# A transformer block in one kernel: low and high limbs of x and ctx in common tiles, one 512-column operand in the first projections

## The chip, the cores and the metric

The kernel runs on one core of a Trainium2 chip. The metric is the device time of one execution in microseconds (us); for the kernel before it is the median of three runs. Engines are named as in the profile: PE is TensorE (PEld its weight loads), DVE VectorE, ACT ScalarE, POOL GpSimd, and SP the queue that issues most loads.

## The reference, cut to what matters

One layer of a latent generator, D = 2048, 256 latent tokens x and 256 context tokens ctx, all in fp32:

```python
sh1, sc1, gt1, sh2, sc2, gt2 = split(silu(c) @ w_mod + b_mod, 6)      # the same of c_ctx for ctx: csh1, csc1
h  = rmsnorm(x,   g_attn) * (1 + sc1)  + sh1
hc = rmsnorm(ctx, g_attn) * (1 + csc1) + csh1
cq, ckv, kr, qn, kn, vn, f = split_columns(h  @ w_in)     # 512, 512, 64, 512, 512, 512, 512 columns
..., ckv_c, kr_c, ..., kn_c, vn_c, ... = split_columns(hc @ w_in)
o_mla = attention of 8 heads, queries from cq, keys and values from ckv, kr and ckv_c, kr_c
o_na  = neighbourhood attention of 4 heads, qn on kn, vn in a window with bias, and on kn_c, vn_c
o_fn  = fourier_mix(f, w_fnet)
x = x + gt1 * (concat(o_mla, o_na, o_fn) @ w_out)
h2 = rmsnorm(x, g_ffn) * (1 + sc2) + sh2
x = x + gt2 * conv_ffn(h2, w_up, conv_w, conv_b, w_down)
return rmsnorm(x, g_final)
```

Keys and values are needed of both streams, queries and Fourier input of x alone. So the columns of kn, ckv and kr are projected for x and ctx together, those of qn, cq and f for x alone.

## The kernel before, in words

**Limbs.** Every fp32 product is made of fp32r matmuls. A value is held as a high limb H (a cast) and a low limb L (the rest), and `mm3` (L116) issues three matmuls: H·H, H·L, L·H, at L117, L118 and L119. `split` (L129) makes the limbs: the cast on ACT (L132), the difference on DVE (L133). Weights come from HBM as fp32 `raw` tiles of 1 MB and are split in two halves into `hl` tiles; there are three buffers of half a tile (tag hl, `limb_tile` L168).

**Order of the weights.** `order` (L139) lists the tiles: the first modulation (m, two per kt) and A, then V 0 to 3, B 0 to 9, F 0 to 3, and those of MLA, of the output projection and of the feed-forward part. `take` (L197) hands out quarter tiles; it splits `look` quarters ahead and has the DMA of each tile issued some tiles ahead (`emit_dma`, L173, on SP). A `raw` tile is a buffer of tag **b8**, of which there are 12 (8 KB per partition, L69). A new b8 tile waits until a buffer is free; the trace shows them handed out in the order in which the program asks. Tag **h8** (L72) has 4 more of that size.

**Stages.**
- *A*, L440 to L464: for each of 16 kt (blocks of 128 rows of D), the modulation's shift and scale (`mod1_mm`, L361, 32 matmuls at L371; transposed at L383), from these the modulated input of the next kt (`mod1_h`, L378), and products of the last kt with 7 column blocks of w_in into 7 PSUM banks (`g1`, L412). Each bank has 512 columns: 256 tokens of x, then 256 of ctx. `mod1_h` makes for x and then for ctx: h on DVE (L404), H on ACT (L405), L on DVE (L406). `hx[m]` holds H and L of x for four kt, [128, 2, 4, 256], in h8; `hc[m]` the same of ctx, in b8. So one block and one kt take six matmuls of 256 columns (L418, L419).
- *V*, `proj_N` (L489): vn of all four groups of 128 tokens, with the tokens as stationary operand and 512 columns of weights streaming.
- *B0, B1*, `proj_T` (L478) with `both`: the last block of ckv, and kr; again 256 + 256 columns (L485, L487). After B1 ctx's input is not used any more, and `hc` is free.
- *Neighbourhood stage*, L643 to L665, seven iterations j: qn of head j (B2 to B5, x alone), from j = 4 cq (`cq_unit`, B6 to B8, then B9), scores (`na_scores`, L625, with a bias T from four small loads that are issued on SP behind the last weight tile asked for, L630), softmax, transposes (`pt_stage`, L590, PE L593) into PT, and PT times vn (`pv_stage`, L597) into mix. `qn` and each `PT` are b8 tiles; so are knH, knL, ckv, vnH, vnL, cq, mix.
- *F*, L707 to L715: f from hx; then the Fourier part mixed with the first products of MLA, MLA's eight heads, the output projection (L867), the feed-forward part.

**The second modulation** (`m2_*`, L226 to L301) is filled in between: gt1, sh2, sc2, gt2 as a sum over 16 kt of weights [128, 1024] times a scalar on DVE (L253 and L255), loaded from POOL's queue (L240). `M2` (L227) orders its eight blocks: gate 1 (blocks 0, 1), sc2 (4, 5), sh2 (2, 3), gate 2 (6, 7). `paced` (L123), called in each `mm3` with its columns, decides when a fill comes. At the end of a gate's block the sum is split and added up over partitions on PE (L287, L288) and to the bias on DVE (L291); the gate's tile is a b8 buffer, loaded on SP (L284) when its first block is summed. For sc2 and sh2 there are eight small matmuls (L277) and a copy. `fill_to(32)` after the first block of output columns (L872) makes sure that gate 1 is there.

The lines that say the most:

```python
def mm3(ps, lH, lL, rH, rL, first, last, skip=False):
    ...
    paced(3 * rH.shape[-1])
...
mm3(accs[i][:, :SEQ], lH, lL, *hsl(hx, kt), first=(kt == 0), last=(kt == KT - 1), skip=True)
g1_last.append(mm3(accs[i][:, SEQ:], lH, lL, *hsl(hc, kt), first=False, last=(kt == KT - 1), skip=True))
```

Of the kernel before, what the change touches and what calls it, by code (L numbers as in the profile page):

```python
# [8 lines left out]
F32R = mybir.dt.float32r  # L9
# [5 lines left out]
P = 128  # L15
D = 2048
KT = 16
# [22 lines left out]
def _columns(*parts):  # L40

    at, o = {}, 0
    for n, w in parts:
        at[n] = (o, o + w)
        o += w
    return at, o
# [2 lines left out]
SM, SM_W = _columns(("ident", 128), ("c1", 16), ("gq", 4), ("gkv", 4), ("gffn", 16), ("bsh2", 16), ("bsc2", 16),  # L49
                    ("conv", 352))  # L50
SA, SA_W = _columns(("c2", 32), ("bm1", 64), ("ga", 32))


@with_exitstack
def block_kernel(ctx: ExitStack, tc: tile.TileContext, a, out):
# [60 lines left out]
    def mm3(ps, lH, lL, rH, rL, first, last, skip=False):  # L116
        pe.matmul(ps, lH, rH, start=first, stop=False, skip_group_check=skip)  # L117
        pe.matmul(ps, lH, rL, start=False, stop=False, skip_group_check=skip)  # L118
        ins = pe.matmul(ps, lL, rH, start=False, stop=last, skip_group_check=skip).ins  # L119
        paced(3 * rH.shape[-1])  # L120
        return ins

    def paced(n):  # L123
        pace[1] += pace[0] * n * 0.427e-3
        if pace[1] >= 1:
            pace[1] -= 1
            fill()
# [96 lines left out]
    gates = {}  # L224

    KIND = ("g", "sh", "sc", "g")  # L226
    M2 = [(blk, kt) for blk in (0, 1, 4, 5, 2, 3, 6, 7) for kt in range(KT)]  # L227
    m2 = {"dma": 0, "acc": 0, "t": {}, "due": None, "age": 0}

    def m2_dma(n):  # L230
# [122 lines left out]


    hx, hc = [None] * 4, [None] * 4
    wt = {}
    bm1 = smv("bm1").rearrange("p (g s j) -> p g s j", g=KT, s=2)
    ga = smv("ga").rearrange("p (g j) -> p g j", g=KT)
# [19 lines left out]
    def mod1_h(kt, sb):  # L378
        with ExitStack() as held:
            for made in g1_last[-1:] if kt else x_made[1:]:  # L380
                held.enter_context(tc.issue_after(made))
            for s in range(2):
                pe.transpose(ms[:, 256 + s * P : 256 + (s + 1) * P], sb[:, s * P : (s + 1) * P], idt)  # L383
            t = tiny(4, "mt")
            tv = t.rearrange("p (s j) -> p s j", s=2)
            quarters_ = ms[:, 256:512].rearrange("p (s r c) -> p s c r", s=2, r=4)[:, :, 0:2, :]
            dve.tensor_reduce(tv, quarters_, AX.X, ALU.add)
        dve.tensor_tensor(tv, tv, bm1[:, kt], ALU.add)
        dve.scalar_tensor_tensor(tv[:, 1], tv[:, 1], 1.0, ga[:, kt], ALU.add, ALU.mult)
        m = kt // 4  # L390
        xk = xT[m][:, kt % 4, :]
        with ExitStack() as held:
            if kt:
                held.enter_context(tc.issue_after(hmade[-1]))
            dve.tensor_tensor(xk, xk, rxb, ALU.mult)
        if hx[m] is None:
            hx[m] = h8([P, 2, 4, SEQ], F32R, s="hx")
            hc[m] = b8([P, 2, 4, SEQ], F32R, s="hc")
        for j, hh in enumerate((hx, hc)):
            xs = xT[m][:, kt % 4, j * SEQ : (j + 1) * SEQ]  # L400
            A, B = tv[:, 1, j : j + 1], tv[:, 0, j : j + 1]
            H, L = hh[m][:, 0, kt % 4, :], hh[m][:, 1, kt % 4, :]
            h32 = b1(s="h32")
            hmade.append(dve.tensor_scalar(h32, xs, A, B, ALU.mult, ALU.add).ins)  # L404
            hx_made.append(act.activation(H, xs, AF.Identity, bias=B, scale=A).ins)  # L405
            dve.tensor_tensor(L, h32, H.bitcast(F32), ALU.subtract)  # L406

    def hsl(hh, kt, lo=0, n=SEQ):
        t = hh[kt // 4]
        return t[:, 0, kt % 4, lo : lo + n], t[:, 1, kt % 4, lo : lo + n]  # L410

    def g1(kt, tiles):  # L412
        for i in tiles:
            if i in (0, 4):
                wt["A"] = take(("A", kt // 2), 2 * (kt % 2) + i // 4)
            w, c0 = wt["A"], (i % 4) * P
            lH, lL = w[:, 0, c0 : c0 + P], w[:, 1, c0 : c0 + P]
            mm3(accs[i][:, :SEQ], lH, lL, *hsl(hx, kt), first=(kt == 0), last=(kt == KT - 1), skip=True)  # L418
            g1_last.append(mm3(accs[i][:, SEQ:], lH, lL, *hsl(hc, kt), first=False, last=(kt == KT - 1), skip=True))  # L419

    def a_limbs(kt, made):

# [55 lines left out]
    def proj_T(key, ps, both, part=None):  # L478

        for kt in range(*((0, KT), (0, KT // 2), (KT // 2, KT))[0 if part is None else part + 1]):  # L480
            k = kt % 4
            if k == 0:
                t = take(key, kt // 4)
            lH, lL = t[:, 0, k * P : (k + 1) * P], t[:, 1, k * P : (k + 1) * P]
            mm3(ps[:, :SEQ], lH, lL, *hsl(hx, kt), first=(kt == 0), last=(kt == KT - 1), skip=True)  # L485
            if both:
                mm3(ps[:, SEQ:], lH, lL, *hsl(hc, kt), first=False, last=(kt == KT - 1), skip=True)  # L487

    def proj_N(kind, toks):  # L489

# [150 lines left out]


    pace[0] = RATES["NA"]  # L643
    qn = b8([P, 2, 4, SEQ], F32R, s="qn")
    es, PTs = {}, {}
    for j in range(7):
        if j < 4:
# [8 lines left out]
        if 1 <= j < 5:  # L656
            es[j - 1] = na_scores(j - 1)
        if 2 <= j < 6:
            PT = PTs[j - 2] = b8([P, 2, 4, SEQ], F32R, s="PT")
            for qt in range(2):  # L660
                pt_stage(es[j - 2][qt], PT, qt)
            es.pop(j - 2)
# [204 lines left out]
    for nb in range(4):  # L867
# [1 line left out]
            if nb or q == 3:  # L869
                wo_unit(nb, q, t_outer=(nb == 3 and q == 3))  # L870
        if nb == 0:
            fill_to(32)  # L872
        for t in range(2):
            x2_cols(nb, t, gates[0], ss2)
        if nb == H_AT:
# [279 lines left out]
```

## Time and profile before

| | |
|---|---|
| median of 3 runs | 1261.91 us (1261.33 to 1263.05) |
| profiled execution | 1260.39 us |
| its span, first to last instruction | 1258.6 us, granted clock 0.995 |
| matmuls, weight loads | 7522 each |
| A stage | from 28 us; V from 144.5, B0 from 189.4, B2 from 212.5, F from 278.4 us |
| loads | 304.76 MB, mean 242 GB/s |

The page gives the busy time of each engine, the chain of work that ended last, groups of instructions by line, and the loads. Other views of the trace are named by what they show: windows (busy time in stretches), the timeline, waits, groups by form. Matmuls overlap, so that the mean of a group is longer than the step from one matmul to the next.

### The profile page before, as it was taken

The page shows a single profiled execution, that of the slowest core. Times are in us where ns is not written, and L with a number is a line of the kernel's source. Part 1 is how long each engine was busy: PE and PEld are TensorE (multiplying, and loading weights), DVE is VectorE, ACT ScalarE, POOL GpSimd, SP SyncE. Part 2 cuts the span into 40 slices and gives each one's busy share as a digit, 9 for nine tenths or more (in the row PEclk, how much of TensorE's full clock was granted, in tenths as well). Part 3 has the DMA queues.
Part 4 walks back from the last instruction along what each step waited for, and adds up shares of the span by engine and source line. Part 5 has one row for each costly group of instructions (what it writes and reads, how often), then busy time and mean ns, then how long its engine had stood idle before and what let it go on. Part 6 is the DMA issues. An engine that isn't in the chain of part 4 may idle for free.

```text
span 1258.6 us, 18991 instructions
## 1 busy us (share of the span) xinstructions
PE 1232.7 (98%) x7522; PEld 1073.0 (85%) x7522; DVE 956.3 (76%) x1408; ACT 634.3 (50%) x976; POOL 113.6 (9%) x175
## 2 busy tenths in 40 slices
PE   5999999999999999999999999999999999999996
PEld 4888889898888888999888888888888888888885
DVE  5455888897999788998888975777766677667785
ACT  4332323664566545666656433555543555445553
POOL 0000121011211112110121500000000000000000
PEclk8999999999999999999999999999999999999999
DMA  9999888674657798744677866555555545555541
GB/s 371 399 395 385 344 300 323 228 289 154 223 204 281 271 377 305 283 168 168 209 261 253 300 230 256 198 173 196 186 186 198 190 178 201 185 187 195 173 197 67
DMA packets 55369, 304.76 MB, mean 242 GB/s; under 512 B 6256, under 2 KB 7408, under 8 KB 29040
## 3 DMA queue, kind: packets, MB, share of 16 engines
q1 hardware_dynamic: 36128, 235.29, 50.9%
q0 software_dynamic: 18432, 67.12, 15.1%
q8 instruction: 59, 0.97, 0.3%
q10 hardware_dynamic: 720, 1.13, 0.2%
q14 instruction: 30, 0.25, 0.1%
HBM read 301.42 MB, written 2.10 MB: 241 GB/s over the span
## 4 chain that ended last, share of the span: by engine, by line
PE 93%; DVE 4%; DMA 1%; ACT 1%; issue 1%; POOL 0%; SPq 0%; DVEq 0%; POOLq 0%; ACTq 0%
PE ps L942 21%; PE ps L118 16%; PE ps L119 16%; PE ps L117 16%; PE ps L943 11%; PE g L117 2%; PE ms L371 2%; PE g L118 2%; PE g L119 2%; DMA x<-in_ctx_dram 1%; PE ps L593 1%; DVE acc L255 1%; DVE hl L133 1%; PE ps L277 1%; DVE xT L331 0%
## 5 line engine op out<-in xcount | busy, mean ns | idle before, releaser
L132 ACT CAST hl<-raw 128x1024 fp32r<-128x1024 f32 (+3 forms) x351 | 363.5, 1036 | 349.7 <-PE ps L119 242.5
L133 DVE TENSOR_TENSOR hl<-raw,hl 128x1024 fp32r<-128x1024 f32 (+3 forms) x351 | 422.0, 1205 | 154.1 <-ACT hl L132 153.6
L942 PE MATMUL ps<-hn,hl 128*128 128x512 f32 x1152 | 405.5, 397 | 0.0
L943 PE MATMUL ps<-hn,hl 128*128 128x256 f32 x1152 | 322.6, 280 | 0.0
L942 PEld LDWEIGHTS ps<-hn,hl 128*128 128x128 f32 x1152 | 216.4, 188 | 53.1
L943 PEld LDWEIGHTS ps<-hn,hl 128*128 128x128 f32 x1152 | 217.3, 189 | 0.1
L255 DVE SCALAR_TENSOR_TENSOR acc<-wm,c,acc 128x1024 f32<-128x1024 f32 x120 | 153.5, 1279 | 6.7 <-DMA wm<-in_wm_dram 6.3
L118 PE MATMUL ps<-hl,act 128*128 128x512 f32 x344 | 133.9, 389 | 0.0
L117 PE MATMUL ps<-hl,act 128*128 128x512 f32 x344 | 133.9, 389 | 0.0
L119 PE MATMUL ps<-hl,act 128*128 128x512 f32 x344 | 133.8, 389 | 0.0
L240 POOL DMA_DIRECT2D wm<-in_wm_dram x128 | 68.2, 533 | 336.4 <-DVE acc L255 247.8
L118 PEld LDWEIGHTS ps<-hl,act 128*128 128x128 f32 x344 | 64.6, 188 | 13.5 <-DVE hl L133 0.2
L117 PEld LDWEIGHTS ps<-hl,act 128*128 128x128 f32 x344 | 64.6, 188 | 13.5
L119 PEld LDWEIGHTS ps<-hl,act 128*128 128x128 f32 x344 | 64.6, 188 | 13.3
L119 PE MATMUL ps<-h,hl 128*128 128x258 f32 x256 | 72.8, 284 | 0.0
L117 PE MATMUL ps<-h,hl 128*128 128x258 f32 x256 | 72.4, 283 | 0.0
L118 PE MATMUL ps<-h,hl 128*128 128x258 f32 x256 | 72.2, 282 | 0.0
L963 ACT ACTIVATE cv<-ps,sm 128x256 f32<-128x256 f32 x88 | 49.8, 567 | 44.5 <-DVE ps L961 43.9
L235 POOL COPY hold<-hl 128x1 f32<-128x1 f32 x36 | 38.1, 1058 | 242.0 <-DVE hl L133 172.8
L964 DVE SCALAR_TENSOR_TENSOR cv<-ps,sm,cv 128x255 f32<-128x255 f32 x88 | 42.1, 480 | 20.0 <-ACT cv L963 20.0
L114 POOL TENSOR_TENSOR r<-v,mhalf 128x1 f32<-128x1 f32 (+1 forms) x3 | 2.7, 895 | 531.5 <-DVE v L113 527.7
L117 PE MATMUL ps<-hl,mix 128*128 128x512 f32 x128 | 50.4, 394 | 0.0
(287 smaller groups left out, 2238.4 us busy)
## 6 DMA issues: line engine op xcount, KB each, us to landing
raw<-in_wup_dram SPq DMA_DIRECT2D x88, 1024.0 KB, 4.9
wm<-in_wm_dram POOLq DMA_DIRECT2D x128, 512.0 KB, 5.3
raw<-in_wdn_dram SPq DMA_DIRECT2D x44, 1024.0 KB, 4.9
raw<-in_wm_dram SPq DMA_DIRECT2D x32, 1024.0 KB, 9.1
raw<-in_wo_dram SPq DMA_DIRECT2D x16, 1024.0 KB, 7.8
raw<-in_wB_dram SPq DMA_DIRECT2D x10, 1024.0 KB, 10.2
raw<-in_wA_dram SPq DMA_DIRECT2D x16, 448.0 KB, 8.4
raw<-in_wV_dram SPq DMA_DIRECT2D x4, 1024.0 KB, 10.4
```

The source lines that it names most:

```text
L117: pe.matmul(ps, lH, rH, start=first, stop=False, skip_group_check=skip)
L118: pe.matmul(ps, lH, rL, start=False, stop=False, skip_group_check=skip)
L119: ins = pe.matmul(ps, lL, rH, start=False, stop=last, skip_group_check=skip).ins
L132: act.copy(H, src)
L133: return dve.tensor_tensor(L, src, H.bitcast(F32), ALU.subtract).ins
L235: hold = pool.tensor_copy(tiny(1, "hold"), recent[0][:, 1, 0:1].bitcast(F32)).ins
L240: pool.dma_start(w, a["wm2"][blk * 16 + kt])
L255: dve.scalar_tensor_tensor(m2["a"], w, c1[:, kt : kt + 1], m2["a"], ALU.mult, ALU.add)
L942: pe.matmul(ps, w[:, 0, k * P : (k + 1) * P], h[:, k].rearrange("p s n -> p (s n)"), start=kt == 0, stop=False, skip_group_check=True)
L943: pe.matmul(ps[:, :SEQ], w[:, 1, k * P : (k + 1) * P], h[:, k, 0, :], start=False, stop=kt == KT - 1, skip_group_check=True)
L963: act.activation(t, ps[:, :SEQ], AF.Identity, bias=c[:, 3:4], scale=c[:, 1:2])
L964: dve.scalar_tensor_tensor(t[:, 1:], ps[:, : SEQ - 1], c[:, 0:1], t[:, 1:], ALU.mult, ALU.add)
```

## The change

The input of the first projections is kept by limb instead of by stream. For each m there are two tiles, `hH` (h8) and `hL` (b8), each [128, 2, 4, 256] with the stream as second index; `hx[m]` and `hc[m]` become views on them (class `Limbs`), and `hsl2` gives the 2 x 256 columns of both streams as one operand. `g1` and `proj_T` with `both` call `mm3` once for 512 columns; `proj_T` for x alone, V and F go through the views as before. `paced` counts the columns of the result.

`hL` holds x's low limb too, so its b8 buffers stay in use to the end of F. `qn` and `PT` take ctx's parts of these tiles (both limbs), after B1 is done with them: qn that of m = 3, PT in turn those of m = 0, 1, 2. In the second modulation sc2's blocks come ahead of gate 1's, and `fill_to(32)` becomes `fill_to(64)`.

```diff
+class Limbs:
+    def __init__(self, H, L):
+        self.limbs = H, L
+
+    def __getitem__(self, at):
+        return self.limbs[at[1]][(at[0],) + tuple(at[2:])]
...
-        paced(3 * rH.shape[-1])
+        paced(3 * ps.shape[-1])
...
-    M2 = [(blk, kt) for blk in (0, 1, 4, 5, 2, 3, 6, 7) for kt in range(KT)]
+    M2 = [(blk, kt) for blk in (4, 5, 0, 1, 2, 3, 6, 7) for kt in range(KT)]
...
+    hxc = [None] * 4
...
-            hx[m] = h8([P, 2, 4, SEQ], F32R, s="hx")
-            hc[m] = b8([P, 2, 4, SEQ], F32R, s="hc")
+            hxc[m] = h8([P, 2, 4, SEQ], F32R, s="hH"), b8([P, 2, 4, SEQ], F32R, s="hL")
+            hx[m], hc[m] = [Limbs(*(t[:, j] for t in hxc[m])) for j in range(2)]
...
+    def hsl2(kt):
+        return [t[:, :, kt % 4, :] for t in hxc[kt // 4]]
...
-            mm3(accs[i][:, :SEQ], lH, lL, *hsl(hx, kt), first=(kt == 0), last=(kt == KT - 1), skip=True)
-            g1_last.append(mm3(accs[i][:, SEQ:], lH, lL, *hsl(hc, kt), first=False, last=(kt == KT - 1), skip=True))
+            g1_last.append(mm3(accs[i], lH, lL, *hsl2(kt), first=(kt == 0), last=(kt == KT - 1), skip=True))
...
-            mm3(ps[:, :SEQ], lH, lL, *hsl(hx, kt), first=(kt == 0), last=(kt == KT - 1), skip=True)
             if both:
-                mm3(ps[:, SEQ:], lH, lL, *hsl(hc, kt), first=False, last=(kt == KT - 1), skip=True)
+                mm3(ps, lH, lL, *hsl2(kt), first=(kt == 0), last=(kt == KT - 1), skip=True)
+            else:
+                mm3(ps[:, :SEQ], lH, lL, *hsl(hx, kt), first=(kt == 0), last=(kt == KT - 1), skip=True)
...
-    qn = b8([P, 2, 4, SEQ], F32R, s="qn")
+    qn = hc[3]
...
-            PT = PTs[j - 2] = b8([P, 2, 4, SEQ], F32R, s="PT")
+            PT = PTs[j - 2] = hc[(j - 2) % 3]
...
-            fill_to(32)
+            fill_to(64)
```

## The prediction

> **What bounds the kernel now.** I read the page's busy times and chain first.
>
> ```profile
> PE 1232.7 (98%) x7522; PEld 1073.0 (85%) x7522; DVE 956.3 (76%) x1408; ACT 634.3 (50%) x976; POOL 113.6 (9%) x175
> PE 93%; DVE 4%; DMA 1%; ACT 1%; issue 1%; POOL 0%; SPq 0%; DVEq 0%; POOLq 0%; ACTq 0%
> ```
>
> TensorE is busy nearly throughout and carries 93% of the chain, so what the change takes from its stream in the first projections is kept, unless something else becomes late there. The windows tell what that could be (columns: window, length, busy of PE, PEld, DVE, ACT, POOL with instruction counts, clock, DMA share, GB/s).
>
> ```profile
> 28.00:60.00 32.00, 31.69 (x324) 26.95 (x328) 16.71 (x42) 10.08 (x19) 0.00 (x0) 0.95 1.01 414
> 60.00:90.00 30.00, 30.00 (x324) 25.32 (x316) 13.69 (x35) 8.74 (x15) 2.84 (x6) 1.00 0.98 387
> 310.00:350.00 40.00, 39.27 (x214) 32.97 (x212) 39.57 (x65) 21.11 (x42) 7.39 (x14) 1.00 0.68 227
> ```
>
> In the A stage, which begins at 28 us, PE is full and the transfers are nearly so: two limits lie close together. From 310 to 350, in the Fourier part and the first heads of MLA, VectorE is 99% busy (39.57 of 40) and PE loses 0.7 us: there a third one is near.
>
> **Term 1, half as many matmuls.** The groups by form count what is joined (one row of the six of the A stage and of the three of ctx in B0 and B1; x and ctx, and L117, L118 and L119, have the same counts):
>
> ```profile
> L117 PE MATMUL g<-hx,hl 128*128 128x256 f32 x112 | 34.6, 314 | 1.8 <-ACT hx L405 1.8
> L117 PE MATMUL ps<-hc,hl 128*128 128x256 f32 x32 | 9.1, 283 | 0.0
> ```
>
> 3 x 112 pairs in the A stage and 3 x 32 in B0 and B1 become one matmul of 512 columns each: 432 matmuls and 432 weight loads go. Durations overlap, so the price is the step from start to start: first B0 (16 steps lie between the two rows), then V, where 512 columns stream already (6 steps).
>
> ```profile
> 189.78 0.28 PE L117 MATMUL ps<-hc,hl 128*128 128x256 f32 x1
> ...
> 191.70 0.28 PE L118 MATMUL ps<-hx,hl 128*128 128x256 f32 x1
> ```
>
> ```profile
> 166.76 0.39 PE L117 MATMUL ps<-hl,hx 128*128 128x512 f32 x1
> ...
> 168.12 0.39 PE L117 MATMUL ps<-hl,hc 128*128 128x512 f32 x1
> ```
>
> 1.92/16 = 0.120 us for 256 columns and 1.36/6 = 0.2267 us for 512. A pair costs 0.240 now and 0.2267 afterwards: 13.3 ns less. 432 x 0.0133 = 5.75 us, of which 336 x 0.0133 = 4.47 in A and 1.28 in B. V's 512 columns are one run, the new operand is two runs of 256 in one tile; the trace has no such operand. Bounds: 0 (two runs cost what two matmuls cost) and 5.75. I take 5.75, since the step in V goes with the column count, and 256 extra columns cost 0.107.
>
> The Trainium skill (TensorE: Matmul & The Clock Gate, section on the back-to-back issue gap) gives a warm step of N/2.4 + 2.5 ns; by that a pair would save 2.5 ns and the change 1.1 us in all. The two rows do not agree: both steps lie 11 ns or more above the rule, and their difference leaves 13.3 ns per matmul.
>
> **Term 2, the start.** The first matmul now needs the high limbs of both streams.
>
> ```profile
> 28.16 0.59 ACT L405 ACTIVATE hc<-xT,mt 128x256 fp32r<-128x256 f32 x1
> 28.31 1.22 PE L117 MATMUL g<-hx,hl 128*128 128x256 f32 x4 [1.85 <-ACT hx L405]
> 29.64 0.42 DVE L406 TENSOR_TENSOR hc<-h,hc 128x256 fp32r<-128x256 f32 x1
> ```
>
> PE started at 28.31, released by hx's cast; hc's ends at 28.75, so it now starts some 0.5 us later. The second matmul of a product needs hc's low limb (30.06); until then there are four tiles' first matmuls, as PE ran L117 x4 first before. Bounds 0.5 and 1.75 (all waits for 30.06); I take 0.5, since the order written for now already puts the four ahead. In later steps of A nothing of this is left: the limbs of a kt are made during the product before.
>
> **Term 3, buffers of the neighbourhood stage.** Tag b8 has 12 buffers, shared with the weight tiles (raw). Before, hc's four come free during B1, and the loads go into them; x's limbs lie in h8. Now b8 holds the low limbs of both streams to the end of F. Against that, qn, PT (one or two at a time) and, until the third block of the second modulation is summed, gate 1 no longer need any. Count at iterations 0 to 2: hL 4, kn 2, ckv, vn 2 = 9, three left for raw (before 7 or 8, so four or five); at 3, mix makes 10; at 4, cq makes 11: one, until the last scores free knH and knL.
>
> ```profile
> SPq L183 <- PE ps L119: 25.0, 6, 8.0
> ```
>
> That row of SP's waits (200 to 300 us: total, times, longest) is those loads, released by matmuls. Afterwards a load waits for the last split of an earlier weight tile. How much time that leaves is read from one tile, B8: its two splits, and PE's first matmuls of B7 and of B8.
>
> ```profile
> 253.08 1.04 ACT L132 CAST hl<-raw 128x1024 fp32r<-128x1024 f32 x1
> 260.84 1.22 DVE L133 TENSOR_TENSOR hl<-raw,hl 128x1024 fp32r<-128x1024 f32 x1
> 255.36 0.36 PE L117 MATMUL ps<-hx,hl 128*128 128x256 f32 x1
> 263.43 0.36 PE L117 MATMUL ps<-hx,hl 128*128 128x256 f32 x1
> ```
>
> A buffer is held for 5.9 us of landing (a row below) and 9.0 from the first split's begin to the last one's end (253.08 to 262.06): 14.9. PE takes a tile every 8.1 us. Two buffers give 16.1 us and suffice, barely; one does not. I followed the buffers in the order in which the program asks for them: B3 gets B0's, B4 to B8 those of B1 to B5, mix that of B6, B9 that of B7, cq and F0 those of knH and knL; with that only one tile has to make do with one buffer. Late is that tile, B9, and with it the four T loads of the last head, which are queued behind it on SP.
>
> ```profile
> 242.44 0.33 SPq L183 DMA_DIRECT2D raw<-in_wB_dram  x1
> 244.26 2.43 SPq L631 DMA_DIRECT2D T<-in_T_dram  x4
> 254.53 7.88 SPq L183 DMA_DIRECT2D raw<-in_wF_dram  x3
> ```
>
> ```profile
> 250.50 1.23 DVE L133 TENSOR_TENSOR hl<-raw,hl 128x1024 fp32r<-128x1024 f32 x1 [0.96 <-ACT hl L132]
> 254.07 0.42 DVE L637 SCALAR_TENSOR_TENSOR S<-ps,T 128x256 f32<-128x256 f32 x1 [0.36 <-PE ps L119]
> ```
>
> ```profile
> DMA to landing us min/median/max: 5.3/5.9/6.3
> ```
>
> ```profile
> 254.34 0.39 PE L119 MATMUL ps<-knH,qn 128*128 128x512 f32 x1
> 262.64 1.04 PE L593 MATMUL ps<-sm,S 128*128 128x128 f32 x8
> ```
>
> B7's last split ends at 251.73, B9 goes out there instead of 242.44, T at 252.1 instead of 244.26, and with T's 5.9 us to landing (that row is of these four) the bias add L637 starts at 258.0 instead of 254.07: 3.9 us late. From there to the transposes L593 there were 8.6 us, with other work between; cq's first write waits for knH (254.73) instead of a free buffer, 2 us, on ACT, with no matmul behind it. B9 itself lands near 258, 5 us ahead of PE's need (one tile after 263.43, less its split). Bounds 0 and 3.9 us of PE at L593; I take 0.7, near the lower end, since the chain holds other work that can go first.
>
> **Term 4, the modulation blocks change places.** The gate's blocks are split and added to the bias; the others are only summed. Per gate block that is on VectorE one split and two adds:
>
> ```profile
> L133 DVE TENSOR_TENSOR acl<-acc,acl x4: 1216/1224/1226, 169.8 to 735.3; 128x1024 fp32r<-128x1024 f32 x4
> L291 DVE TENSOR_TENSOR gate<-ps,gate x8: 680/682/691, 182.3 to 749.7; 128x512 f32<-128x512 f32 x8
> L849 DVE TENSOR_TENSOR tm<-ps,gate x40: 681/684/692, 438.2 to 1249.0; 128x512 f32<-128x512 f32 x40
> ```
>
> ```profile
> 233.94 1.28 DVE L291 TENSOR_TENSOR gate<-ps,gate 128x512 f32<-128x512 f32 x2
> 235.14 0.75 DVE L637 SCALAR_TENSOR_TENSOR S<-ps,T 128x256 f32<-128x256 f32 x2
> 245.49 0.66 PE L593 MATMUL ps<-sm,S 128*128 128x128 f32 x4 [1.30 <-ACT S L587]
> 299.76 0.75 DVE L253 TENSOR_SCALAR acc<-wm,c 128x1024 f32<-128x1024 f32 x1
> 351.10 0.75 DVE L253 TENSOR_SCALAR acc<-wm,c 128x1024 f32<-128x1024 f32 x1
> ```
>
> So 2.6 us per block leave V and the neighbourhood stage, where the adds stood just ahead of a softmax (L637) that PE later waited 1.30 us for; up to 1.3 us is gained. They come back after the third block (the fourth's first product stands at 299.76) and after the fourth (the fifth's at 351.10): the first block's adds fall into 310 to 350, where VectorE has 0.4 us free, and up to 1.4 us is lost there; the second's split and adds come after that window. I take 0, bounds -1.3 and +1.4. The gate's own load is one SP issue (0.33 us, as B9's), once b8 has emptied. Waiting for 64 products instead of 32 at the first output column costs nothing: the gate's first reader L849 starts at 438.2, 87 us after they are summed.
>
> The pace of the fills is unchanged: one call with 512 columns instead of two with 256.
>
> **Sum.** -5.75 + 0.5 + 0.7 + 0 = -4.55 us. The profiled execution took 1260.39 us (span 1258.6 and 1.8 around it), so 1255.8; it lies 1.5 under the median of the runs, 1261.91, which is what is compared: 1257.4, I say 1257.3. By the bounds of terms 2 to 4 at full term 1: -5.75 + 0.5 - 1.3 = -6.55 (1255.4) to -5.75 + 1.75 + 3.9 + 1.4 = +1.3 (1263.2). Some 0.2% (2.5 us) is what a measurement of this kernel tells from no change.
>
> **Rivals.** *Transfers set the pace of A.* One kt takes 7.31 us:
>
> ```profile
> 81.05 1.86 PE ms L371 x32
> 88.36 1.86 PE ms L371 x32
> ```
>
> 21 pairs take 0.28 from it, so 387 GB/s must become 387 x 7.31/7.03 = 402. If 387 were the limit, A would keep its length: -1.28 + 0.5 + 0.7 = -0.1, 1261.8. For it: share 0.98. Against it: 414 GB/s in the window from 28 to 60, and the lead that the loads have.
>
> ```profile
> L183 SPq DMA_DIRECT2D raw<-in_wm_dram x1: 328/328/328, 118.7 to 118.7; - x1
> DMA to landing us min/median/max: 6.5/6.5/6.5
> 132.21 1.07 PE L371 MATMUL ms<-raw,cs 128*32 128x256 f32 x16
> ```
>
> The last tile of the first modulation goes out at 118.7 and lands 6.5 later, at 125.2; the sixteen matmuls of the tile ahead of it start at 132.21, its own behind them: a lead of 7 us, more than the 4.47 to be saved. Chance 0.08. The Trainium skill (DMA: Bandwidth & Descriptors, section "Where 436 GB/s comes from") says that the HBM's share of a core, about 358 GB/s, binds loads; by that A could not get shorter. The window with 414 does not agree.
>
> *Two runs cost what two matmuls cost.* Then the change does not do what it says: term 1 is 0 and the sum +1.2, 1263.1. For it: no row has such an operand. Against it: in V the step grows by no more than the columns. Chance 0.08. With the 1.1 us of the Trainium skill's step (TensorE: Matmul & The Clock Gate, the section named above) as term 1 it would be 1262.0.
>
> *Too few b8 buffers, slower.* If one buffer alone serves the weight tiles over a stretch, each tile takes 14.9 us against PE's 8.1: 6.8 us lost per tile. Two such tiles, B9 and F0: 13.6 - 4.6 = +9, 1271. It decides from the point where knH and knL are not free yet when F0 is asked for, or cq and mix are given buffers ahead of the loads. Against it: their last reader starts at 254.34, and F0 went out at 254.53 even now. Chance 0.12.
>
> **Chances and range.** The forecast 0.72, of which 0.61 beyond 0.2%, 0.08 within, 0.03 slower; the first two rivals 0.16, all within; the third 0.12, slower. Faster 0.61, same 0.24, slower 0.15. Range 1255.0 to 1263.1: the forecast's bounds (with half a us of spread below) and the first two rivals.
>
> **What would show it.** In A and B0, B1 rows of 128x512 with 112 and 32 per line, steps of 0.227; a kt of 7.03 us; V some 4 us earlier; the last head's T out after B7's last split, and L637 just behind its landing; the adds L291 past 300. Steps of 0.24, or a kt of 7.3 with idle before L371 on raw, would make it wrong, as would holes of several us on PE ahead of the splits of B8 to F3.

## The result, and the profile after

The changed kernel took 1270.49 us (median of 4 runs, 1268.90 to 1271.04) beside 1261.68 (1261.33 to 1263.05, 4 runs): a ratio of 1.0068, 95% interval 1.0056 to 1.0080, 8.8 us slower. The forecast was 1257.3 in a range of 1255.0 to 1263.1. The profiled execution took 1270.80 us, with a span of 1269.0 and a granted clock of 0.989 (before: 1258.6 and 0.995). Lines of the changed kernel are numbered 10 to 15 higher: `mm3` L127 to L129, `split` L142 and L143, the weight loads L193, the products of the second modulation L263 and L265, the small sums L287 (eight in the program, sixteen rows in the profile), the gate's adds L301, the transposes L608, the T loads L646, the bias add L652.

The page's busy times and chain:

```profile
PE 1234.5 (97%) x7090; PEld 1051.8 (83%) x7090; DVE 956.5 (75%) x1408; ACT 635.0 (50%) x976; POOL 114.5 (9%) x175
PE 90%; DVE 4%; DMA 3%; issue 2%; ACT 1%; SPq 0%; POOL 0%; DVEq 0%; POOLq 0%; ACTq 0%
```

The 432 matmuls are gone (7522 to 7090), but PE's share of the chain fell from 93% to 90%, and DMA's rose from 1% to 3%: PE waits more. The groups by form show the joined operand as expected, and two idle times that are new or larger:

```profile
L127 PE MATMUL g<-hH,hl 128*128 128x512 f32 x112 | 45.1, 429 | 2.3 <-ACT hH L416 2.3
L127 PE MATMUL ps<-hH,hl 128*128 128x512 f32 x32 | 12.6, 393 | 0.0
L287 PE MATMUL ps<-ones_r,acc 128*128 128x2 f32 x64 | 8.6, 265 | 1.6 <-DVE acc L265 1.6
L608 PE MATMUL ps<-sm,S 128*128 128x128 f32 x32 | 5.1, 297 | 6.7 <-ACT S L602 6.7
```

The windows (columns as in the prediction; the clock is the number ahead of the DMA share):

```profile
28.00:60.00 32.00, 30.82 (x220) 21.45 (x220) 16.46 (x41) 10.42 (x19) 0.00 (x0) 0.91 1.00 403
60.00:90.00 30.00, 30.00 (x248) 20.71 (x249) 14.60 (x38) 9.22 (x16) 3.52 (x6) 1.00 0.98 388
160.00:180.00 20.00, 18.44 (x75) 15.24 (x74) 12.23 (x12) 3.16 (x3) 4.24 (x8) 0.83 0.74 268
240.00:280.00 40.00, 34.78 (x266) 33.73 (x267) 33.09 (x59) 27.98 (x54) 3.18 (x6) 0.96 0.58 198
310.00:350.00 40.00, 39.02 (x200) 32.52 (x199) 39.94 (x63) 20.26 (x38) 6.89 (x13) 1.00 0.69 233
```

The kernel before has, in the third and the fourth of them:

```profile
160.00:180.00 20.00, 20.00 (x90) 16.57 (x89) 15.54 (x14) 5.17 (x5) 4.57 (x9) 1.00 0.84 302
240.00:280.00 40.00, 38.70 (x302) 37.07 (x301) 35.56 (x65) 27.55 (x53) 6.31 (x8) 1.00 0.75 274
```

From 60 to 90 us PE is still full. The loss shows in two windows: from 160 to 180 PE is idle for 1.6 us and its clock stands at 0.83, and from 240 to 280 it is idle for 5.2 us, where before it was idle for 1.3. Where it was lost is read by setting the same matmul of both timelines side by side (us from the span's start):

| first matmul of | before | after | shift |
|---|---|---|---|
| the second modulation product | 33.28 | 34.79 | +1.51 |
| V | 144.46 | 143.25 | -1.21 |
| B0 | 189.43 | 194.07 | +4.64 |
| B2 | 212.46 | 217.68 | +5.22 |
| B4 | 225.37 | 230.58 | +5.21 |
| B5 | 234.93 | 243.11 | +8.18 |
| B7 | 255.36 | 263.12 | +7.76 |
| B8 | 263.43 | 274.51 | +11.08 |
| F | 277.80 | 288.88 | +11.08 |
| after F (its last matmul) | 302.12 | 311.36 | +9.24 |
| the output projection | 406.19 | 416.63 | +10.44 |
| the end | 1258.6 | 1269.0 | +10.4 |

So 2.72 us are gained in A and 1.84 in F. V loses 5.85 us. B0 and B1 lose 0.58: the wide operand gives some 1.3 there, and the second block of sc2 now has its small matmuls there (1.84 us from 208.36). The neighbourhood stage loses 5.86, of which 2.97 from B4 to B5 and 3.32 from B7 to B8, and the stretch from the end of F to the output projection 1.20. With the 1.51 of the start this is the whole shift of the end: 1.51 - 2.72 + 5.85 + 0.58 + 5.86 - 1.84 + 1.20 = 10.4. The medians differ by 8.8 only, since the profiled execution of the kernel before lies 1.3 us under its median and that of the changed kernel 0.3 over it. The hole in V (a hole is idle time of PE), on PE:

```profile
164.57 0.39 PE L129 MATMUL ps<-hl,hL 128*128 128x512 f32 x1
166.51 3.09 PE L287 MATMUL ps<-ones_r,acc 128*128 128x2 f32 x16 [1.56 <-DVE acc L265]
169.46 0.77 PE L127 MATMUL ps<-hl,hH 128*128 128x512 f32 x1
170.03 0.63 PE L128 MATMUL ps<-hl,hH 128*128 128x512 f32 x1
...
173.02 0.63 PE L129 MATMUL ps<-hl,hL 128*128 128x512 f32 x1
173.45 0.61 PE L127 MATMUL ps<-hl,hH 128*128 128x512 f32 x1
173.88 0.42 PE L128 MATMUL ps<-hl,hH 128*128 128x512 f32 x1
```

and on VectorE at that time:

```profile
162.84 1.28 DVE L265 SCALAR_TENSOR_TENSOR acc<-wm,c,acc 128x1024 f32<-128x1024 f32 x1 [2.29 <-DMA wm<-in_wm_dram]
164.05 1.22 DVE L143 TENSOR_TENSOR hl<-raw,hl 128x1024 fp32r<-128x1024 f32 x1
165.18 1.28 DVE L265 SCALAR_TENSOR_TENSOR acc<-wm,c,acc 128x1024 f32<-128x1024 f32 x1
```

The block that ends here is now one of sc2, and the program asks for its sum in the very next fill, while a gate's block is summed seven fills after its end. VectorE had waited 2.29 us for a modulation load, so the block's last product ended at 166.46; PE, in order, stood 1.56 us for it. Then the sixteen matmuls took 3.09 us (1.84 at full clock), and the steps from 170.03 to 173.45 are 3.42/8 = 0.43 us instead of 0.227: half the clock.

The neighbourhood stage: SP's waits from 200 to 300 us and its timeline, then the bias add and the transposes of heads 0 and 3.

```profile
SPq L193 <- DVE hl L143: 73.1, 9, 16.3
```

```profile
214.77 9.10 SPq L193 DMA_DIRECT2D raw<-in_wB_dram  x2
223.93 3.27 SPq L646 DMA_DIRECT2D T<-in_T_dram  x4
...
259.15 0.33 SPq L193 DMA_DIRECT2D raw<-in_wB_dram  x1
259.59 2.38 SPq L646 DMA_DIRECT2D T<-in_T_dram  x4
```

```profile
232.69 0.43 DVE L652 SCALAR_TENSOR_TENSOR S<-ps,T 128x256 f32<-128x256 f32 x1 [2.28 <-DMA T<-in_T_dram]
...
267.59 0.42 DVE L652 SCALAR_TENSOR_TENSOR S<-ps,T 128x256 f32<-128x256 f32 x1 [0.73 <-DMA T<-in_T_dram]
```

```profile
239.33 0.66 PE L608 MATMUL ps<-sm,S 128*128 128x128 f32 x4 [1.45 <-ACT S L602]
242.34 0.90 PE L608 MATMUL ps<-sm,S 128*128 128x128 f32 x3 [2.36 <-ACT S L602]
...
272.02 0.66 PE L608 MATMUL ps<-sm,S 128*128 128x128 f32 x4 [1.46 <-ACT S L602]
274.10 0.66 PE L608 MATMUL ps<-sm,S 128*128 128x128 f32 x4 [1.42 <-ACT S L602]
```

Of the kernel before, T of head 0 and the wait ahead of that head's transposes (those of head 3 stand in the prediction):

```profile
210.15 2.54 SPq L631 DMA_DIRECT2D T<-in_T_dram  x4
```

```profile
234.51 0.66 PE L593 MATMUL ps<-sm,S 128*128 128x128 f32 x4 [0.49 <-ACT S L587]
```

A weight load now waits for the split of an earlier tile (73.1 us of SP's time), and the T loads stand behind it. Those of head 0 go out at 223.93 instead of 210.15, those of head 3 at 259.59 instead of 244.26. The bias add of each waits for them, and PE for the softmax: 3.8 us at head 0, where it was 0.5, and 2.9 us at head 3, where it was nothing.

### The profile page after: what moved, and what is told of

It is laid out like the page before. It is cut to its first block, busy times and chain, and to the rows that moved or that the text cites. A ratio compares the mean times of both kernels' runs of the same rounds, so it can differ in the third digit from the quotient of the medians.

```text
span 1269.0 us, 18125 instructions
## 1 busy us (share of the span) xinstructions
PE 1234.5 (97%) x7090; PEld 1051.8 (83%) x7090; DVE 956.5 (75%) x1408; ACT 635.0 (50%) x976; POOL 114.5 (9%) x175
## 4 chain that ended last, share of the span: by engine, by line
PE 90%; DVE 4%; DMA 3%; issue 2%; ACT 1%; SPq 0%; POOL 0%; DVEq 0%; POOLq 0%; ACTq 0%
PE ps L957 21%; PE ps L127 16%; PE ps L128 16%; PE ps L129 16%; PE ps L958 11%; PE ms L382 2%; PE g L127 2%; PE g L128 2%; PE g L129 2%; DMA T<-in_T_dram 1%; DVE acc L265 1%; DMA x<-in_ctx_dram 1%; PE ps L608 1%; DVE hl L143 1%; PE ps L287 1%
## 5 line engine op out<-in xcount | busy, mean ns | idle before, releaser
L143 DVE TENSOR_TENSOR hl<-raw,hl 128x1024 fp32r<-128x1024 f32 (+3 forms) x351 | 422.2, 1204 | 168.1 <-ACT hl L142 167.4
L142 ACT CAST hl<-raw 128x1024 fp32r<-128x1024 f32 (+3 forms) x351 | 363.6, 1036 | 363.0 <-PE ps L129 258.0
L265 DVE SCALAR_TENSOR_TENSOR acc<-wm,c,acc 128x1024 f32<-128x1024 f32 x120 | 153.4, 1278 | 2.8 <-DMA wm<-in_wm_dram 2.3
L127 PE MATMUL ps<-hl,act 128*128 128x512 f32 x344 | 133.8, 389 | 0.0
L129 PE MATMUL ps<-hl,act 128*128 128x512 f32 x344 | 133.8, 389 | 0.0
L127 PEld LDWEIGHTS ps<-hl,act 128*128 128x128 f32 x344 | 64.6, 188 | 13.5
L129 PEld LDWEIGHTS ps<-hl,act 128*128 128x128 f32 x344 | 64.6, 188 | 13.4
L129 PE MATMUL ps<-h,hl 128*128 128x258 f32 x256 | 72.8, 284 | 0.0
L127 PE MATMUL ps<-h,hl 128*128 128x258 f32 x256 | 72.4, 283 | 0.0
L127 PE MATMUL ps<-hl,mix 128*128 128x512 f32 x128 | 50.4, 394 | 0.0
```

The source lines that it names most:

```text
L142: act.copy(H, src)
L143: return dve.tensor_tensor(L, src, H.bitcast(F32), ALU.subtract).ins
L265: dve.scalar_tensor_tensor(m2["a"], w, c1[:, kt : kt + 1], m2["a"], ALU.mult, ALU.add)
```

## The experiments

Theory: the operand brings its gain, and three things that the change brings along cost more: the sums of sc2 asked for too soon (V), T behind weight tiles that wait for buffers, and the gate's adds in the stretch where VectorE is full. Rivals: the weight tiles have too few buffers, so T is a symptom; the order of the blocks costs nothing; the gain is not there. In what follows a time in us with a ratio behind it is the median of the timed runs, with the ratio to the kernel before (taken over all timed executions, so it is not exactly the quotient of two medians) and its 95% interval; all else is from the one profile.

**Sums late.**

```diff
-            m2["due"], m2["age"] = (blk, acc), SUM_LAG
+            m2["due"], m2["age"] = (blk, acc), 0
```

> Edit: the changed kernel, but the sums of a block of sc2 or sh2 come seven fills after the block's end, as the gate's did, and no longer in the next fill. Theory (a new wait in V, and a lower clock behind it): in the changed kernel PE stood 1.56 us at the first such sum for VectorE, its sixteen matmuls took 3.1 us where before they took 1.84, and some ten 512-column steps took 0.43 instead of 0.227. With the sum late all three go: 1.6 + 1.3 + 2.1 = 5.0 us, so about 1265.5, and B0 begins near 189 us as before. Rival (the sixteen small matmuls themselves bring the clock down, the wait has no part in it): only the 1.6 us go, 1268.9, and the 0.43 steps stay in the trace. Rival (the time comes back as later waits for T): 1270.

1270.14 us (1.0066, 1.0051 to 1.0081): no gain. Yet V did what the theory says: B0 begins at 189.06, and from 160 to 180 PE is full at clock 1.00:

```profile
160.00:180.00 20.00, 20.00 (x98) 16.82 (x97) 17.17 (x17) 4.21 (x4) 5.80 (x11) 1.00 0.88 301
```

with the sixteen matmuls in that stretch, in 1.84 us. So small matmuls alone do not lower the clock. What V gave was lost behind it, at places the timeline names:

```profile
267.18 1.11 PE L608 MATMUL ps<-sm,S 128*128 128x128 f32 x4 [3.16 <-ACT S L602]
...
268.30 0.41 PE L128 MATMUL ps<-hL,hl 128*128 128x256 f32 x1
...
516.28 1.54 PE L876 MATMUL ps<-sm,x 128*128 128x128 f32 x6 [1.66 <-DVE x L865]
518.57 1.01 PE L127 MATMUL ps<-h,hl 128*128 128x258 f32 x3 [0.74 <-ACT h L142]
```

T is late as before (a hole of 3.16, and steps of 0.21 for 256 columns behind it). And the last sum of sh2, which the edit made late too, now stands just ahead of the row at 516.28, at the end of the output projection. At B2 PE stood 6.9 us ahead of the changed kernel (210.82 beside 217.68), at the start of the output projection still 4.4 (412.21 beside 416.63), and at its last matmul 0.3 behind (1259.31 beside 1259.01). So the rival, that the time comes back as waits for T, explains at most 2.4 us of the loss; the 4.7 behind the output projection's start go with the sum of sh2. The edit was too broad; that the two blocks of sh2 should have been left alone is shown further down.

**T early.** The four loads of a head are issued an iteration earlier:

```diff
+        if 1 <= j < 5:
+            na_T(j - 1)
         if j < 4:
             ps = bank()
...
-        T = b2((P, 2, SEQ), s="T")
...
+        T = Ts.pop(h)
```

> Edit: the changed kernel, but each head's four T loads are issued one iteration earlier, ahead of the weight tile behind which they stood. Theory (the T loads, queued behind weight tiles that wait for a buffer, are what the softmaxes of heads 0 and 3 come late for): the losses of PE at the transposes, 2.98 us after B4 and 3.32 us after B7, go: about 1264.2, and the window 240 to 280 has PE at 38.5 of 40 instead of 34.8. Rival (the weight tiles themselves have too few buffers; with T out of the way PE waits for the splits of B6 or B9 instead): 1269 to 1271, idle time of PE ahead of the first product of a tile.

1262.38 us (1.0010, 0.9996 to 1.0023): 8.1 us less than the changed kernel and 1.8 less than the theory's 1264.2. The buffers and the order of the weight loads are as they were, and PE waits for no weight tile, so T is the cause of the holes of heads 0 and 3 and the weight tiles are not. In the window PE has 39.12 us:

```profile
240.00:280.00 40.00, 39.12 (x312) 37.77 (x311) 34.35 (x61) 26.88 (x53) 6.30 (x8) 1.00 0.66 227
```

The hole in V is still there in this profile, but its consequence is not:

```profile
166.14 1.95 PE L287 MATMUL ps<-ones_r,acc 128*128 128x2 f32 x16 [1.70 <-DVE acc L265]
167.95 0.48 PE L127 MATMUL ps<-hl,hH 128*128 128x512 f32 x1
168.27 0.39 PE L128 MATMUL ps<-hl,hH 128*128 128x512 f32 x1
168.50 0.40 PE L129 MATMUL ps<-hl,hL 128*128 128x512 f32 x1
```

A hole of 1.70 us, and the steps behind are 0.23: full clock. So whether a hole of this length halves the clock differs from one execution to the next, which goes with the spread of this kernel's runs: 1259.04 to 1266.73 in 10 runs, beside 1260.22 to 1262.97 in 19 of the kernel before. It also means that some of the 8.1 us may be the clock and not T: between the two profiles V is 3.0 us shorter (47.80 us from its first matmul to B0's, beside 50.82), and the stretches B4 to B5 and B7 to B8 are 4.8 us shorter (6.29 more than in the kernel before, now 1.45 more).

**kt 0 apart.**

```diff
+            if kt == 0:
+                mm3(accs[i][:, :SEQ], lH, lL, *hsl(hx, kt), first=True, last=False, skip=True)
+                g1_last.append(mm3(accs[i][:, SEQ:], lH, lL, *hsl(hc, kt), first=False, last=False, skip=True))
+                continue
```

> Edit: the changed kernel, but the products of kt 0 alone are made as before, 256 columns of x and 256 of ctx apart. Theory (the first product waits for the high limbs of both streams, and the slow first steps then hold for twice the columns): the 1.5 us by which the second modulation product begins later than before go, 336 - 21 pairs stay joined (0.3 us): -1.2 us, 1269.3. Rival (the slow steps at the start last a set time after PE's first product, whatever it does): the start moves by 0.5 to 0.9 us only and the sum is -0.4, 1270.1, which is hardly to be told from no change.

1271.64 us (1.0083, 1.0055 to 1.0111; 1269.08 to 1277.22): no gain. In the profile the second modulation product began at 33.22 (changed kernel 34.79), but that is taken up again below.

**The three together.**

> Edit: the changed kernel with the three edits together (sums late, T early, kt 0 apart). Theory (three added waits, each independent of the others, hide a gain that is there): 5.0 + 6.3 + 1.2 = 12.5 us less than the changed kernel, 1258.0, that is 3.7 us or 0.3% under the kernel before. Rival (the gain of the wide operand is itself lost later, where VectorE is full in the Fourier part and MLA): not under the kernel before, 1261 to 1263.

1264.59 us (1.0022, 1.0013 to 1.0032), not 1258.0. In the profile PE stood 1.0 us ahead of the kernel before at the output projection, and 4.1 us behind it in the feed-forward part: the sums of sh2 again. In the two kernels with late sums V has no hole, and between them T early took 5.5 us (1270.14 to 1264.59; kt 0 apart, which they do not share, turns out to be worth nothing below): that is the cleaner price of the late T.

**Two edits**: T early, and late sums for sc2 alone.

```diff
-            m2["due"], m2["age"] = (blk, acc), SUM_LAG
+            m2["due"], m2["age"] = (blk, acc), 0 if blk in (4, 5) else SUM_LAG
```

> Edit: the changed kernel with T issued early, and the sums of the two sc2 blocks seven fills late; those of sh2 stay in the next fill, and kt 0 stays joined. Theory: with all three edits PE stood at -1.0 us against the kernel before when the output projection began and at +4.1 at the end of it and of the step behind it, since the last sum of sh2, now late too, was waited for there (holes of 1.7 and 0.7 us, then 1.7 us of slow steps). With sh2 as it was these 5.1 us stay saved: 1264.6 - 5.1 = 1259.5, 2.1 us or 0.17% under the kernel before. Rival (that stretch has become slow by the clock, whatever the sum does): 1264.

1259.60 us (0.9983, 0.9974 to 0.9992), as the theory had it. With both waits gone the change is 2.1 us faster than the kernel before. Beside the kernel with T early alone, the late sums of sc2 are worth 2.8 us.

**The order of the blocks alone**, in the kernel before.

```diff
-    M2 = [(blk, kt) for blk in (0, 1, 4, 5, 2, 3, 6, 7) for kt in range(KT)]
+    M2 = [(blk, kt) for blk in (4, 5, 0, 1, 2, 3, 6, 7) for kt in range(KT)]
...
-            fill_to(32)
+            fill_to(64)
```

> Edit: the kernel before with nothing of the change but the order of the modulation blocks (sc2 ahead of gate 1) and the wait for 64 products at the first output column. Theory (the wait of the sums in V comes from the order, not from the wide operand): V gets longer by the 1.6 us hole, the small matmuls (1.84 for 0.93) and up to 3.5 us of low clock, the second block's sums add 0.9 in B; 1.84 come back in F, and some 1.2 us are lost in MLA where the gate's adds now lie: 1263.5 without the low clock to 1267 with it. Rival (VectorE has the sums ready in time when the operand is not wide, the order costs nothing): 1261.5, or 1260.3 if the adds' leaving the softmaxes is worth something.

1269.74 us (1.0066, 1.0052 to 1.0079): these two lines, with no wide operand and no shortage of buffers, cost 8.0 us, more than the theory's 5.

```profile
166.03 0.39 PE L119 MATMUL ps<-hl,hc 128*128 128x512 f32 x1
170.53 2.60 PE L277 MATMUL ps<-ones_r,acc 128*128 128x2 f32 x16 [4.12 <-DVE acc L255]
```

The hole is 4.12 us here, since VectorE waited 4.76 us for a modulation load ahead of the block's last products. So the wait is in the end one of a transfer that everything else had hidden.

**The old order in the changed kernel** (the reverse of those two lines).

> Edit: the changed kernel, but with the modulation blocks in the order of before (gate 1 first) and the wait for 32 products. Theory (the order was the price of the buffers): V has no hole any more and B0 begins about 1.2 us earlier than before; but the gate's tile then holds a b8 buffer from V on, two are left for weight tiles until mix is asked for, one until cq, and the splits of B6 to F0 come late: holes of 5 us and more on PE between B4 and F, 1275 (from 1268 to 1285). Rival (the order is nothing but a loss, the buffers suffice anyhow): 1264 to 1265, the changed kernel less V's 5.9.

1277.64 us (1.0127, 1.0113 to 1.0141): V has no hole, B0 begins at 188.35, but the gate's tile takes a b8 buffer, and PE now waits for the softmaxes of heads 0 and 3:

```profile
237.93 1.11 PE L608 MATMUL ps<-sm,S 128*128 128x128 f32 x4 [6.71 <-ACT S L602]
240.64 0.69 PE L608 MATMUL ps<-sm,S 128*128 128x128 f32 x2 [1.59 <-ACT S L602]
274.75 1.11 PE L608 MATMUL ps<-sm,S 128*128 128x128 f32 x4 [3.83 <-ACT S L602]
277.42 0.90 PE L608 MATMUL ps<-sm,S 128*128 128x128 f32 x3 [1.56 <-ACT S L602]
```

The time is near what the theory gave, the place only in part: PE waited for the softmaxes, not for the splits of B6 to F0. So in the changed kernel as it stands the new order was worth paying for. Which part of these holes is T behind the weight tiles (the bias adds of head 0 waited 1.9 and 1.4 us for T) and which the gate's adds on VectorE in the same place (1.28 us from 234.64) was not told apart. Nor was the old order run with T early, which may do without the new one.

**T early in the kernel before**, as a control.

> Edit: the kernel before, with nothing of the change, but each head's T loads issued one iteration earlier. Theory (in the kernel before T comes in time; what the early T gives in the changed kernel is the cure of a wait that the change made): no change, 1261.5, between 1260.7 and 1262.3; PE's losses at the transposes, 0.7 and 1.5 us, stay, since the softmax chain is what they wait for. Rival (an early T is worth something by itself, so part of the gain of the version with two edits is not the change's): 2 us less, 1259.6.

1260.72 us (0.9995, 0.9986 to 1.0004): no change that can be told. So most of what T early gives the changed kernel, 5.5 to 8.1 us, is the cure of a wait that the change made.

**Two edits, and kt 0 apart.**

> Edit: the version with T early and the sc2 sums late, and in addition the products of kt 0 as 256 columns of x and 256 of ctx apart. Theory (the wide first product costs the start some 1.5 us): 0.7 to 1.2 us less than the 1259.6 of that version, 1258.6, with the second modulation product starting within 0.5 us of the kernel before's 33.28. Rival (the length of the slow first stretch is a matter of the clock and goes from 2.9 to 5.9 us whatever the width): no change, 1259.6; in the two runs so far that had kt 0 apart that start was 33.22 and 34.95.

1259.81 us (0.9989, 0.9981 to 0.9998), beside 1259.60 without: no change, as the rival had it. The second modulation product began at 34.66 here. In the kernels that keep two operands throughout it began at 33.28, 33.46, 34.41, 34.49 and 35.74; with kt 0 apart at 33.22, 34.66 and 34.95; with all joined at 34.25 to 35.70 in six. So this start scatters by 2.5 us with two operands already, and a price of the wide first product does not stand out of that, but for a longer wait ahead of it, which is taken up under term 2 below.

**Two edits, and other rates of the fills.**

```diff
-RATES = dict(A=0.18, V=0.55, B=0.3, NA=0.21, F=0.135, FN=0.464, MLA=0.292, O=0.226, UP=0.132, DN=0.3)
+RATES = dict(A=0.18, V=0.55, B=0.3, NA=0.21, F=0.135, FN=0.34, MLA=0.33, O=0.226, UP=0.132, DN=0.3)
```

> Edit: the version with T early and the sc2 sums late, and the modulation's fills made rarer in the Fourier part (0.464 to 0.34) and more frequent in MLA (0.292 to 0.33). Theory (the gate's adds, now in the stretch where VectorE is full, are what costs 1.2 us between F and the output projection): four products of 0.75 to 1.2 us leave that stretch, and 0.6 to 1.2 us come back: 1258.7. Rival (the holes there, 0.75 and 1.45 us ahead of a split, are those of one late split each and not of the sum of the work): no change, 1259.6, or a hole moved to another head.

1257.74 us (0.9966, 0.9954 to 0.9979): 1.9 us less than with two edits, where the theory had 0.9, 4.0 us under the kernel before, and the fastest of all. From 310 to 350 VectorE now has 1.6 us to spare, and PE is full:

```profile
310.00:350.00 40.00, 40.00 (x215) 34.30 (x214) 38.38 (x64) 21.56 (x42) 6.33 (x12) 1.00 0.68 217
```

**The new order in the kernel before, with sc2's sums late.**

> Edit: the kernel before with the new order of the modulation blocks, and the sc2 sums seven fills late. Theory (all that the order costs, 8.0 us, is the wait for the sum and what the wait brings with it): 1261.7 to 1262.9, the kernel before plus at most the 1.2 us of the gate's adds in MLA, and V without a hole. Rival (the order costs by itself, by the work that VectorE gets at other places): 1264 to 1268.

1264.29 us (1.0022, 1.0012 to 1.0033): of the 8.0 us that the order costs there, 5.4 were the wait and what it brought, and 2.6 stay, more than the 1.2 allowed for. In the profile 2.1 of them lie between the end of F and the output projection, where the gate's adds now are: a hole of 1.40 us of PE waiting for the Fourier part's split, where the kernel before has 0.33, and one of 1.29 at 355.52, where it has none. The theory's "all" is refuted; the order has a second price.

**The rates alone**, in the kernel before.

> Edit: the kernel before, with nothing of the change, but the fills of the second modulation rarer in the Fourier part and more frequent in MLA (0.464 to 0.34, 0.292 to 0.33), as in the fastest version so far (1257.7). Theory (these rates mend only what the new order of the blocks brought into that stretch; the kernel before has holes of 0.49 and 0.55 us there): 0 to 1.0 us less, 1261.2, so that at least 3 of the 4 us of the fastest version are the change's own, once its waits are removed. Rival (the rates are worth the same without the change): 2 us less, 1259.7.

1261.18 us (0.9995, 0.9986 to 1.0004), as the theory had it. Between the two kernels with these rates lie 3.4 us by the medians (1257.74 and 1261.18) and 3.7 by the ratios: that is the change with its waits removed, T early included, of which the control left at most 1.8 us (0.9986) to T itself.

## Why the prediction was wrong, by its own steps

*What bounds the kernel.* Right: PE is the bound, and what leaves its stream is kept "unless something else becomes late". Two things did.

*Term 1, -5.75: right in kind, too large by 1.1 to 1.7.* In B0 the step of the new operand is V's, and in A it is a little longer (22 steps lie between the first two rows, 12 between the last two):

```profile
199.74 0.39 PE L128 MATMUL ps<-hL,hl 128*128 128x512 f32 x1
...
204.73 0.39 PE L129 MATMUL ps<-hH,hl 128*128 128x512 f32 x1
...
85.60 0.40 PE L129 MATMUL g<-hH,hl 128*128 128x512 f32 x1
...
88.36 0.39 PE L129 MATMUL g<-hH,hl 128*128 128x512 f32 x1
```

4.99/22 = 0.2268 and 2.76/12 = 0.230. A pair in A gives 0.240 - 0.230 = 10 ns, 336 x 0.010 = 3.4, with B's 1.28 4.7 us. (With the sums out of the way, B0 to B2 took 21.76 us instead of 23.03: the 1.28.) A kt takes 7.10 or 7.12 us (starts of the modulation product at 74.45, 81.55 and 88.67), not 7.03. Read from the whole stretch A gives less: from the second modulation product to V the changed kernel takes 108.46 us instead of 111.18, 2.72 less, since its first 11 us gain nothing (34.79 to 46.01, beside 33.28 to 44.45). These two lengths are the same within 0.02 us in all profiles with the joined operand throughout (six) and with two operands (five). So A and B gave 4.0 to 4.7 us. Two runs of 256 columns thus cost nearly what one of 512 does (0.2268 and 0.230, beside 0.2267), and that rival falls. The transfers did not set A's pace either: PE is full from 60 to 90 us with 388 GB/s beside it, the kt is shorter, and from 90 to 120 and 120 to 145 us the loads went at 394 and 407 GB/s, where before they went at 389 and 391; so that rival falls too. The Trainium skill's 358 GB/s (DMA: Bandwidth & Descriptors, the section named in the prediction) agrees as little with these 388 as with the 414 before. The section works that figure out as half of what two cores share, and this kernel runs on one core. The Trainium skill's N/2.4 + 2.5 ns (TensorE: Matmul & The Clock Gate, section on the back-to-back issue gap) is given there for an isolated matmul; for streams of weight loads and matmuls the section has about 131 ns at 512 columns, and the 227 and 230 ns here agree with neither figure.

*Term 2, +0.5: right as far as the wait goes.* PE's wait ahead of its first product was 1.85 us and is 2.34:

```profile
29.18 2.93 PE L127 MATMUL g<-hH,hl 128*128 128x512 f32 x6 [2.34 <-ACT hH L416]
```

It is 1.84 or 1.85 in all eight profiles with two operands in the first kt and 2.33 or 2.34 in all six with one: 0.49 us. The rest of the +1.5 lies behind it, in the slow steps of the start, whose length scatters by more than that; in the timed runs no experiment tells the term from nothing.

*Term 3, +0.7: the step that failed, mis-sized.* "I take 0.7, near the lower end, since the chain holds other work that can go first." The queue was followed rightly: B9 was to go out at 251.73 and did at 259.15, that is 251.4 when PE's shift of 7.76 is taken off; the bias add was to start at 258.0, and its two starts, 265.31 and 267.59, are 257.6 and 259.8 by the same measure. But the end of this chain is PE's, and nothing absorbed the delay: 3.3 us, close to the upper bound of 3.9. And "Late is that tile, B9, and with it the four T loads of the last head" was incomplete: head 0's T stands behind B6, whose buffer comes free with B3's last split (223.53), and cost another 3.0. The question asked was whether the weight tiles come in time, which they did; what was queued behind them had less room. So the term was 6.3 us in the profile (2.97 and 3.32) instead of 0.7, and T early took 8.1 us out of the changed kernel and 5.5 out of the one with late sums.

*Term 4, 0: the step that failed, a wait not seen.* "The gate's blocks are split and added to the bias; the others are only summed" counted VectorE's work and not PE's wait. A gate's block is summed seven fills after its end, a block of sc2 in the next one; moved to V, where the modulation loads come late, that puts PE behind VectorE and VectorE behind a load. V lost 5.85 us in the profile: 1.6 of hole, 2.0 where small matmuls stand for the gate's wide ones (2.95 from 166.51 to the next start at 169.46, for 0.9), the rest, some 2.2, steps at half the clock. None of it was within the bounds of -1.3 and +1.4. The upper bound itself was about right for what it was made for: from the end of F to the output projection 1.2 us were lost, and with other rates of the fills 1.9 us came back. But the place was another: "the second's split and adds come after that window" put them at no cost, and it is behind that split (358.12, 1.22 us on VectorE) that PE waits 1.29 us for a weight split, at 361.32.

*The rival "too few b8 buffers, slower", 1271* had the time (1270.5) by luck, and not the cause. It let PE wait for tiles, 6.8 us each; no tile was late, and T early cured it with the buffers as they were. Its 14.9 us per buffer were too short besides: the 5.9 us of landing are those of T, and the weight tiles of B landed in 9.0 us (median of eight from 160 to 300 us, in the kernel before).

What stays open: how much of each loss is the wait and how much the clock behind it, since the clock differs between executions of the same kernel; why the first 11 us of A behind the second modulation product gain nothing, and why A's step is 0.230 and B's 0.2268; and whether the old order of the modulation blocks would do with T early.

## What to carry to other kernels

When buffers get scarce, ask of each queue not only whether the big loads still come in time, but what small load stands behind them and how soon it is needed. When steps of a planner are reordered, take over each step's own delay: a sum that was harmless at once in one stage needs its seven fills in another, where its input waits for a transfer. And a gain of 0.3% may be hidden whole behind waits that come with the change, so undo them one by one before it is dropped: the kernel with them removed ran 4.0 us under the one before, and 3.4 under the one before with the same rates.

## What was not expected of the hardware

Short holes on PE can cost more than themselves. After 1.56 us of waiting the sixteen two-column matmuls of the changed kernel took 3.09 us instead of 1.84, and the ten steps behind them went at half the granted clock; after 1.70 us with T early, and 1.73 with kt 0 apart, they did not; after 4.12 us with the order alone they did, and so did the steps behind the 2.36 us hole at 242.34 of the changed kernel, where steps of 256 columns then took 0.21 for 2 us. Over all fourteen profiles, and behind the start, the granted clock was read over the 2 us that begin 1 us after each hole. Behind the 19 holes of 0.88 to 1.29 us it was 1.00 each time; behind six of the 23 from 1.30 to 1.75 us it was 0.50; behind seven of the eight from 2.02 to 6.71 us it was 0.50 or 0.51. So a hole of some 1.3 to 2 us may or may not halve the clock, and the same sixteen small matmuls stood behind holes that did and holes that did not.

The Trainium skill (TensorE: Matmul & The Clock Gate, the part on the HAM clock gate) has the clock follow a free-running window of about 3.4 us, which would make it a matter of chance whether a hole shorter than the window counts; the mixed outcome between 1.30 and 1.75 us agrees with that. It names idle windows of that length as the condition, and here holes of less than half of it were enough in some cases; what else decides is not shown.

In the same way the half clock at the start lasted, over the fourteen profiles, from 2.9 us (28.31 to 31.25, the kernel before) to 5.9 us (28.66 to 34.58, the three edits together) after PE's first product, and the width of that product did not decide it: it was 2.9 to 5.9 us with 256 columns and 3.6 to 5.7 with 512.
